# Which pairs of products run in turns, when the token operands are made, and a fifth weight buffer for part of the run

## The chip, the core and the metric

The kernel runs on one core of a Trainium2 chip. The metric is the time of one execution on the device in microseconds (us), the median of several runs. Five engines take part, each with its own queue of instructions that it works off in order: PE (TensorE, matrix products), DVE (VectorE) and ACT (ScalarE) for elementwise work, POOL (GpSimd) and SP (SyncE), which here only issue DMA transfers.

## What is computed

One block of a hybrid encoder, 2048 tokens of 1024 features, all in float32:

```python
h    = rmsnorm(x, norm_g)
proj = h @ W_in            # 1024 -> 6144 columns, 48 column tiles of 128
q, k, v, z_att, gb, gc, u, z_conv, g_att, g_conv = split(proj)
att    = chunked_rel_attention(q, k, v, rel_bias)        # 8 heads, own chunk + 8 before
y_att  = (att * silu(z_att)) @ w_att_out
vconv  = causal_depthwise_conv(gc * u, conv_w, conv_b)   # width 3
y_conv = (gb * vconv * silu(z_conv)) @ w_conv_out
m      = sigmoid(g_att) * y_att + sigmoid(g_conv) * y_conv
out    = rmsnorm(x + m @ w_out, final_norm_g)
```

## The kernel before

**Products.** The tokens are taken in two halves of 1024. The 48 column tiles of `W_in` are taken in 24 *pairs*: 8 gate pairs (numbers 0 to 7), 8 conv pairs (8 to 15), 4 pairs of q and k (16 to 19), 2 of v and 2 of z. A pair on a half is a 2 by 2 block product (two column tiles, two chunks of 512 tokens, and the 1024 features in two blocks of 512), done with seven block products in the place of eight. They are called by the numbers 1, 2, 6, 5, 7, 4, 3, which is the order in `ORDER` (L36). Each needs a *token operand* (a sum or difference of blocks of tokens, made once for a half by `operand_steps`, L348, one of its seven steps for each product number) and a *weight operand* (the same of weight blocks, made for every pair by `operand`, L375). Every operand is split into a high and a low part, ACT making the high one by a cast and DVE the low one by a subtraction (L122 and L123 for weights, L128 and L129 for tokens). `passes` (L132) runs a product as 12 matmuls: for each of four row blocks high by high, high by low, low by high, so that the third matmul is the first that needs the low part of the weights.

**The stages.** The first three pairs of half 0 (`PLAIN`) are computed from tokens that are not normalized yet, as twelve plain groups of 24 matmuls (in the text q0 to q11; L655 on), each scaled afterwards (`scaled`, L605: DVE reads the PSUM tile `ps_p` and frees its bank). Beside them `between` (L630) normalizes the tokens and makes the first five steps of the token operands. Then `seq` (L561 to L564) gives the order of all other products: half 0 pair by pair but for its last two pairs, which run in turns (`ending`), then the first two pairs of half 1 in turns (`beginning`), then the rest. `names` is the order of the pairs, n the place of a pair in it (0 to 23 in half 0, 24 to 47 in half 1). Half 0 splits the weights and stores them (`wc_d`); in half 1 they are loaded from there, but for the three plain pairs, which are split again. The token operands of half 1 are made by the same `operand_steps`, one step two products after the last product that reads the same operand of half 0 (`due`, L776): both halves share 56 slots (`tt`). After pair n = 28 the attention starts (L777): 131 units of it are spread evenly over the products that are left. Then come the two output products.

**What sets the order.** A scheduler lays down each engine's queue when the kernel is built; in the plain stage the order on PE, DVE and ACT is as written (`manual_schedule`, L646). Four buffers hold weight operands (`wr`, L94); one comes free when its product has run and its store to `wc_d` has landed. PSUM has three banks for products (`ps_d`), so a product waits until the product three places ahead has been read out (*evicted*), by ACT for number 1 (L745) and by DVE otherwise (L749 to L769). For v pairs a turn through PE (`vt`, L433) and a split into `vst` (L440 on ACT, L441 on DVE) follow, for q and k a split (L410, L411), for z a SiLU (L453, L454).

## Time and profile before

| What | Value |
|---|---|
| Median of 3 runs | 1554.11 us (1553.26 to 1556.15) |
| The profiled execution, on the device | 1557.6 us |
| Its span, first to last instruction | 1555.8 us |
| PE busy, share of the span | 1516.6 us, 97% |
| DVE busy | 1039.7 us, 67% |
| ACT busy | 680.1 us, 44% |
| Mean granted PE clock | 0.992 of full speed |

PE is busy nearly all the time, so what can be won lies in its waits and in the stretches at a lower clock. In the timeline a row gives start and length; what stands in square brackets is how long the engine had been idle and what ended that.

### The profile page before, as it was taken

Reading aid. Unit: us, or ns where it says so; the run is one execution under the profiler, and the core shown is the slowest. Engines: PE = TensorE matmul, PEld = TensorE weight load, DVE = VectorE, ACT = ScalarE, POOL = GpSimd, SP = SyncE. Lnnn points to the kernel's source line nnn. Section 1 sums busy time; section 2 is a strip of 40 time slices with the busy share of each in tenths; the row PEclk is TensorE's granted clock in tenths of the full one; section 3 lists DMA queues with packets and bytes.
Section 4 is the critical chain, followed back from the end, with each engine's and each line's share of the span. In section 5 each row is a group of like instructions: output and inputs, shape, how many; then the busy total and the mean of one; then the engine's idle time right before and its main releaser. Section 6 shows DMA issues by size and latency. Waiting matters only on the chain.

```text
span 1555.8 us, 21590 instructions
## 1 busy us (share of the span) xinstructions
PE 1516.6 (97%) x7396; PEld 1267.9 (81%) x7396; DVE 1039.7 (67%) x2078; ACT 680.1 (44%) x1250; POOL 155.0 (10%) x294
## 2 busy tenths in 40 slices
PE   9899999999998999999999999999999999999997
PEld 6678888888776788888888888888888888888886
DVE  7977789796668654666666767677755574445544
ACT  6353353443325343555666556666665231112111
POOL 0000000000000001223222222322220000000000
PEclk9999999999999999999999999999999999999999
DMA  5288999988987835999898776888889945365131
GB/s 209 77 285 307 339 353 327 364 310 305 319 301 262 279 122 177 329 339 341 294 290 272 228 265 228 262 261 272 263 278 322 304 162 200 102 233 193 62 109 68
DMA packets 159406, 389.45 MB, mean 250 GB/s; under 512 B 19904, under 2 KB 40384, under 8 KB 159296
## 3 DMA queue, kind: packets, MB, share of 16 engines
q1 hardware_dynamic: 129088, 302.06, 56.2%
q0 software_dynamic: 20992, 69.22, 13.6%
q10 hardware_dynamic: 9216, 16.78, 2.9%
q8 instruction: 59, 0.97, 0.3%
q14 instruction: 51, 0.42, 0.1%
HBM read 236.99 MB, written 150.99 MB: 249 GB/s over the span
## 4 chain that ended last, share of the span: by engine, by line
PE 83%; DVE 9%; ACT 2%; DMA 2%; issue 2%; POOL 0%; SPq 0%; ACTq 0%; DVEq 0%; POOLq 0%
PE ps_d L137 20%; PE ps_d L135 20%; PE ps_d L136 20%; PE ps_d L876 4%; PE ps_d L874 4%; PE ps_d L875 4%; PE ps_s L190 4%; PE po L228 4%; PE ps_t L210 3%; DVE ptl L216 1%; DVE ps_s L196 1%; DMA wc<-wc 1%; DVE xs L304 1%; ACT pr L200 1%; DMA vv<-v 0%
## 5 line engine op out<-in xcount | busy, mean ns | idle before, releaser
L200 ACT ACTIVATE pr<-ps_s,nmax 128x640 f32<-128x640 f32 (+4 forms) x128 | 93.4, 730 | 96.7 <-DVE nmax L196 96.1
L158 POOL DMA_DIRECT2D q<-q x128 | 66.7, 526 | 681.3 <-DVE wc L123 602.5
L196 DVE CUSTOM_DVE_ANT_0 ps_s<-ps_s,bs 128x640 f32<-128x640 f32 (+4 forms) x128 | 95.4, 745 | 53.8 <-PE ps_s L190 53.2
L122 ACT CAST wc<-wraw 128x512 fp32r<-128x512 f32 x120 | 73.6, 621 | 114.2 <-PE ps_d L137 94.2
L202 ACT ACTIVATE pr<-pr,rs 128x640 f32<-128x640 f32 (+4 forms) x128 | 97.8, 764 | 27.3 <-DVE rs L201 27.2
L190 PE MATMUL ps_s<-kk,q 128*128 128x320 f32 (+1 forms) x448 | 97.4, 333 | 2.9 <-ACT pr L200 2.8
L135 PE MATMUL ps_d<-mid,wy 128*128 128x512 f32 x256 | 99.6, 389 | 0.0
L136 PE MATMUL ps_d<-mid,wy 128*128 128x512 f32 x256 | 99.6, 389 | 0.0
L137 PE MATMUL ps_d<-mid,wy 128*128 128x512 f32 x256 | 99.6, 389 | 0.0
L216 DVE TENSOR_TENSOR ptl<-ps_t,pth 128x640 fp32r<-128x640 f32 (+4 forms) x128 | 94.3, 736 | 6.6 <-ACT pth L215 6.0
L215 ACT CAST pth<-ps_t 128x640 fp32r<-128x640 f32 (+4 forms) x128 | 80.0, 625 | 41.0 <-PE ps_t L210 40.0
L123 DVE TENSOR_TENSOR wc<-wraw,wc 128x512 fp32r<-128x512 f32 x120 | 82.2, 689 | 13.7 <-ACT wc L122 13.5
L210 PE MATMUL ps_t<-ident,pr 128*128 128x128 f32 x560 | 83.9, 276 | 1.1 <-DVE ptl L216 0.6
L883 ACT ACTIVATE sq<-y 128x512 f32<-128x512 f32 x32 | 20.2, 632 | 146.0 <-DVE y L878 141.3
L228 PE MATMUL po<-pth,vv 128*128 128x256 f32 x336 | 79.1, 271 | 1.8 <-DMA vv<-v 1.6
L228 PE MATMUL po<-ptl,vv 128*128 128x256 f32 x336 | 78.3, 281 | 0.2 <-DVE ptl L216 0.2
L874 PE MATMUL ps_d<-wo,mh 128*128 128x512 f32 x192 | 74.7, 389 | 0.0
L875 PE MATMUL ps_d<-wo,mh 128*128 128x512 f32 x192 | 74.7, 389 | 0.0
L876 PE MATMUL ps_d<-wo,ml 128*128 128x512 f32 x192 | 74.7, 389 | 0.0
L190 PEld LDWEIGHTS ps_s<-kk,q 128*128 128x128 f32 x448 | 67.0, 190 | 7.8 <-ACT pr L200 7.4
L878 DVE SCALAR_TENSOR_TENSOR y<-ps_d,y 128x512 f32<-128x512 f32 x32 | 22.1, 692 | 76.0 <-PE ps_d L876 75.9
L210 PEld LDWEIGHTS ps_t<-ident,pr 128*128 128x128 f32 x560 | 63.2, 140 | 11.4 <-DVE ptl L216 2.1
(370 smaller groups left out, 4183.8 us busy)
## 6 DMA issues: line engine op xcount, KB each, us to landing
wc<-wc SPq DMA_DIRECT2D x294, 512.0 KB, 4.8
wraw<-wp_in SPq DMA_DIRECT2D x54, 512.0 KB, 5.9
q<-q POOLq DMA_DIRECT2D x128, 128.0 KB, 4.9
gl<-gate SPq DMA_DIRECT2D x64, 256.0 KB, 3.2
mid<-mid SPq DMA_DIRECT2D x64, 256.0 KB, 5.2
bs<-bias POOLq DMA_DIRECT2D x32, 320.0 KB, 7.2
gate<-c ACTq DMA_DIRECT2D x34, 256.0 KB, 4.7
v<-vst SPq DMA_DIRECT2D x64, 128.0 KB, 4.7
```

Of the source, the lines that this page charges most:

```text
L135: nc.tensor.matmul(ps, lhsT=w[:, 0, k, :], rhs=rh[:, cs], start=(first and k == 0), stop=False)
L136: nc.tensor.matmul(ps, lhsT=w[:, 0, k, :], rhs=rl[:, cs], start=False, stop=False)
L137: nc.tensor.matmul(ps, lhsT=w[:, 1, k, :], rhs=rh[:, cs], start=False, stop=(last and k == len(rhs) - 1))
L190: nc.tensor.matmul(ps[:, i, :m], lhsT=q[s][:, g * P:(g + 1) * P], rhs=kk[:, k1 - n + i * m:k1 - n + (i + 1) * m], start=(s == 0), stop=(s ...
L196: nc.vector.tensor_tensor_reduce(out=view, in0=view, in1=bv, scale=-0.125, scalar=3.0e38, op0=ALU.add, op1=ALU.min, accum_out=nmax)
L200: nc.scalar.activation(out, view, AF.Exp, bias=nmax, scale=-1.0, accum_out=rs)
L210: nc.tensor.transpose(out=ps[:, j * P:(j + 1) * P], in_=pr[:, j * P:(j + 1) * P], identity=ident)
L216: nc.vector.tensor_sub(lo[:, js, qs], src, hi[:, js, qs].bitcast(F32))
L228: nc.tensor.matmul(ps[:, (g0 + a) * P:(g0 + b) * P], lhsT=vv[:, g0 + j, :], rhs=s[:, j, a * P:b * P], start=(i == 0 and s is pt[0]), stop= ...
L874: nc.tensor.matmul(ps, lhsT=mh[:, gs], rhs=wh, start=(k == 0), stop=False)
L875: nc.tensor.matmul(ps, lhsT=mh[:, gs], rhs=wl, start=False, stop=False)
L876: nc.tensor.matmul(ps, lhsT=ml[:, gs], rhs=wh, start=False, stop=(k == KT - 1))
```

## The change

Six things change.

First, the order of half 0: gate pairs 4 and 5 move ahead of the conv pairs, and the last two gate pairs stand behind the first two couples of conv pairs, so that four conv pairs now follow each other at the end. In half 1 gate pair 5 comes at the start, with 3 and 4.

Second, the pairs that run in turns: in half 0 no longer the last two but the first two behind the plain products (n = 3 and 4), and at the start of half 1 three in the place of two (`BEGIN`).

Third, the token operands of half 0: two steps stay in the plain stage (at q6 and q7), and the other five are made beside the pairs in turns, one before every second product.

Fourth, those of half 1: `due` is now a list of places counted from the change of halves (product -5, -4, -1, 2, 5, 7 and 11), and their temporary `t1` comes from the pool of weight sums.

Fifth, a fifth weight buffer: from n = 16 to n = 38 every fifth weight operand is put in an extra pool (`more`), and operands are made or loaded three products ahead there, also in half 0. The memory is that of the convolution's tiles (`cva`), which are opened only while conv pairs run. Ahead of that the same memory holds one raw weight tile (`extra`), since two pairs in turns need more raw tiles at a time; raw tiles of pair 4 are requested at the start.

Sixth, the attention starts one pair later (n = 29), and the pool for gates opens one pair later.

```diff
+BEGIN = 3
-    wtile = lambda name: wr.tile([P, 2, 4, P], F32R, tag="w", name=name)
+    ring = [0, wr]
+
+    def wtile(name):
+
+        ring[0] += 1
+        w = ring[1] if ring[0] % 5 == 0 else wr
+        return w.tile([P, 2, 4, P], F32R, tag="w", name=name)
...
-    conv_stack = ExitStack()
-    cva = conv_stack.enter_context(tc.tile_pool(name="cva", bufs=2))
+    spare = ExitStack()
+    extra = spare.enter_context(tc.tile_pool(name="extra", bufs=1))
+    pools = []
...
-                    t1 = e("t1")
+                    t1 = s_pool.tile([P, 4, P], F32, tag="s1", name="t1").rearrange("p k c -> p (k c)") if half else e("t1")
...
-        r = ww.tile([P, 2, 4, P], F32, tag="w", name="wraw")
+        r = (extra if (p, n) == (names[PLAIN + 2], 0) else ww).tile([P, 2, 4, P], F32, tag="w", name="wraw")
...
-    order = [[*range(G, G + 4), *conv_gate(G + 4, G + 5, G + 6, G + 7), *range(Q, Q + 8)]]
-    order.append([G + 3, G + 4, *range(G, G + PLAIN), *range(Q, Q + 8), *conv_gate(), G + 5, G + 6, G + 7])
+    order = [[*range(G, G + 6), *conv_gate(G + 6, G + 7), *range(Q, Q + 8)]]
+    order.append([G + 3, G + 4, G + 5, *range(G, G + PLAIN), *range(Q, Q + 8), *conv_gate(), G + 6, G + 7])
...
-    both = [(i, k) for i in (6, 5, 7, 4, 3) for k in range(2)]
-    ending = [(1, 0), (2, 0), (6, 0), (1, 1), (2, 1), (6, 1), *both[2:]]
-    beginning = [(1, 0), (2, 0), (1, 1), (2, 1), *both]
-    mid0, mid1 = names[PLAIN:NPAIR - 2], names[NPAIR + 2:]
-    seq = [(p, i) for p in mid0 for i in ORDER]
-    seq += together(*names[NPAIR - 2:NPAIR], ending)
-    seq += together(*names[NPAIR:NPAIR + 2], beginning)
-    seq += [(p, i) for p in mid1 for i in ORDER]
+    beginning = [(i, k) for k in range(BEGIN) for i in (1, 2)]
+    beginning += [(i, k) for i in (6, 5) for k in range(BEGIN)]
+    beginning += [(i, k) for k in range(BEGIN) for i in (7, 4)]
+    beginning += [(3, k) for k in range(BEGIN)]
+    seq = together(names[PLAIN:PLAIN + 2], [*((i, k) for k in range(2) for i in (1, 2)), *((i, k) for i in ORDER[2:] for k in range(2))])
+    seq += [(p, i) for p in names[PLAIN + 2:NPAIR] for i in ORDER]
+    change = len(seq)
+    seq += together(names[NPAIR:NPAIR + BEGIN], beginning)
+    seq += [(p, i) for p in names[NPAIR + BEGIN:] for i in ORDER]
+    due = [change + d for d in (-5, -4, -1, 2, 5, 7, 11)]
...
+    for k in range(2):
+        load_raw(4, k)
...
-        if q > 5 and len(built) < 5:
+        if q in (6, 7):
             built.append(next(steps))
...
+        if n == PLAIN + 3 and i == 1:
+            spare.close()
+            pools[:] = [spare.enter_context(tc.tile_pool(name="cva", bufs=2))]
+        if n == 16 and i == 1:
+            spare.close()
+            ring[1] = spare.enter_context(tc.tile_pool(name="more", bufs=1))
+        elif n == NPAIR + BEGIN + PLAIN + 8 and i == 1:
+            ring[1] = wr
+            spare.close()
+            pools[:] = [spare.enter_context(tc.tile_pool(name="cva", bufs=2))]
...
-        ahead = 3 if half else 2
+        ahead = 3 if half or ring[1] is not wr else 2
...
-        if half == 0 and len(built) < 7 and s:
+        if half == 0 and len(built) < 7 and s % 2:
             built.append(next(steps))
```

How the queues read at the three places that the prediction speaks of. A row is the line, the operation, and the tile written and the tiles read; the numbers in the names tell tiles of one name apart.

**DVE in the plain stage.** Before, from the read-out of q5 (`c_980`) to the first low part of the weights of q9 (`w0_1041`):

```order
L607 TENSOR_TENSOR c_980<-ps_p_891,rb_836 128x512
L123 TENSOR_TENSOR w0_984<-wraw_538,w0_984 128x512
L123 TENSOR_TENSOR w0_987<-wraw_538,w0_987 128x512
L607 TENSOR_TENSOR plain_763<-plain_763,rb_909 128x512
L607 TENSOR_TENSOR plain_823<-plain_823,rb_909 128x512
L129 TENSOR_TENSOR t20l_1018<-xs_523,t20h_1017 128x512
L129 TENSOR_TENSOR t21l_1022<-xs_523,t21h_1021 128x512
L129 TENSOR_TENSOR t22l_1026<-xs_523,t22h_1025 128x512
L129 TENSOR_TENSOR t23l_1030<-xs_523,t23h_1029 128x512
L607 TENSOR_TENSOR c_1033<-ps_p_933,rb_909 128x512
L123 TENSOR_TENSOR w0_1041<-wraw_540,w0_1041 128x512
```

In the changed kernel the same read-out (`c_984`) is followed by one more sum of tokens, then by the same rows down to `t20l`; from there to the first low part of the weights of q9 (`w0_1045`):

```order
L364 TENSOR_TENSOR xs_517<-xs_517,xs_528 128x512
L137 TENSOR_TENSOR t21l_1026<-xs_523,t21h_1025 128x512
L401 TENSOR_TENSOR s2_1251<-s1_1250,wraw_542 128x512
L137 TENSOR_TENSOR t22l_1030<-xs_523,t22h_1029 128x512
L406 TENSOR_TENSOR wraw_544<-wraw_542,wraw_544 128x512
L137 TENSOR_TENSOR t23l_1034<-xs_523,t23h_1033 128x512
L622 TENSOR_TENSOR c_1037<-ps_p_937,rb_913 128x512
L366 TENSOR_TENSOR xs_523<-xs_523,xs_517 128x512 x2
L137 TENSOR_TENSOR t60l_1207<-xs_517,t60h_1206 128x512
L366 TENSOR_TENSOR xs_523<-xs_523,xs_517 128x512 x2
L137 TENSOR_TENSOR t61l_1212<-xs_517,t61h_1211 128x512
L131 TENSOR_TENSOR w0_1045<-wraw_540,w0_1045 128x512
```

The read-out of q6 (`c_1033`, now `c_1037`) stands thirteenth behind that of q5 where it was ninth, and the low part of q9's weights twentieth where it was tenth; the steps for `t5` and `t7`, which stood between the read-outs of q7, q8 and q9, have moved behind the plain stage.

**ACT at the end of the q and k pairs.** Before, in the last of these pairs (n = 19): `hi` is the split of a result, `wc_4043`, `wc_4062` and `wc_4083` are the weights of its products 7, 4 and 3, `wc_4106` those of the next pair's product 1:

```order
L122 CAST wc_4043<-wraw_3820 128x512
L410 CAST hi_4103<-c22_4100 128x512
L122 CAST wc_4062<-wraw_3820 128x512
L122 CAST wc_4083<-wraw_3818 128x512
L122 CAST wc_4106<-wraw_3986 128x512
L410 CAST hi_4124<-u_4016 128x512
```

In the changed kernel (`wc_4030`, `wc_4056`, `wc_4074` are the weights of 7, 4 and 3, `wc_4095` those of the next pair's product 1; `v_4093` is the result of product 3):

```order
L130 CAST wc_4030<-wraw_3837 128x512
L130 CAST wc_4056<-wraw_3837 128x512
L130 CAST wc_4074<-wraw_3835 128x512
L420 CAST hi_4115<-c22_4112 128x512
L420 CAST hi_4136<-u_4028 128x512
L420 CAST hi_4166<-v_4093 128x512
L130 CAST wc_4095<-wraw_4003 128x512
L130 CAST wc_4118<-wraw_4003 128x512
```

The weights of product 4 no longer stand behind the split of product 7's result; the weights of the next pair's product 1 now stand behind the split of product 3's.

**DVE at the change of halves.** Before, in the two z pairs at the end of half 0 (`wc_4766`, `wc_4786` and `wc_4833` are weights of their products 7 and 4):

```order
L129 TENSOR_TENSOR t63l_4763<-xs_1594,t63h_4762 128x512
L123 TENSOR_TENSOR wc_4766<-wraw_4522,wc_4766 128x512
L123 TENSOR_TENSOR wc_4786<-wraw_4321,wc_4786 128x512
L760 TENSOR_TENSOR c22_4803<-v_4744,ps_d_4789 128x512
L761 TENSOR_TENSOR u_4557<-u_4557,ps_d_4789 128x512
L360 TENSOR_TENSOR t1_4809<-xs_1603,xs_1594 128x512
L454 SCALAR_TENSOR_TENSOR sz_4806<-sz_4806,c22_4803 128x512
L360 TENSOR_TENSOR t1_4815<-xs_1603,xs_1594 128x512
L129 TENSOR_TENSOR t50l_4812<-t1_4809,t50h_4811 128x512
L360 TENSOR_TENSOR t1_4821<-xs_1603,xs_1594 128x512
L129 TENSOR_TENSOR t51l_4818<-t1_4815,t51h_4817 128x512
```

In the changed kernel the steps for `t5` and `t7` stand in half 1, ahead of the read-out of the second of its products (`c11_4965`, from bank `ps_d_4951`):

```order
L366 TENSOR_TENSOR xs_1590<-xs_1590,xs_1587 128x512
L137 TENSOR_TENSOR t52l_4984<-t1_4981,t52h_4983 128x512
L370 TENSOR_TENSOR t1_4987<-xs_1596,xs_1587 128x512
L366 TENSOR_TENSOR xs_1590<-xs_1590,xs_1587 128x512 x2
L137 TENSOR_TENSOR t53l_4990<-t1_4987,t53h_4989 128x512
L137 TENSOR_TENSOR t70l_5047<-xs_1593,t70h_5046 128x512
L137 TENSOR_TENSOR t71l_5051<-xs_1593,t71h_5050 128x512
L137 TENSOR_TENSOR t72l_5055<-xs_1593,t72h_5054 128x512
L777 TENSOR_TENSOR c11_4965<-u_4947,ps_d_4951 128x512
L137 TENSOR_TENSOR t73l_5059<-xs_1593,t73h_5058 128x512
```

Between the read-out of the last pair's product 7 (`c22_4862`) and `c11_4965` stand 27 other instructions of this size on DVE. No split of weights is among those behind the last three products of half 0.

## Rows read from the trace of the kernel before

**Rows 1.** Waits of PE: line, waited for, us in total, times, longest.

```profile
PE ps_p L135 <- DVE c L607: 9.1, 3, 3.6
PE ps_d L137 <- DVE wc L123: 6.0, 4, 3.6
PE ps_s L190 <- ACT pr L200: 2.8, 8, 0.6
```

**Rows 2.** Timeline of PE, plain stage: the three waits, two neighbouring matmuls.

```profile
60.09 0.47 PE L135 MATMUL ps_p<-rawh,w 128*128 128x512 f32 x1 [2.46 <-DVE c L607]
...
61.07 0.63 PE L135 MATMUL ps_p<-rawh,w 128*128 128x512 f32 x1
61.50 0.63 PE L136 MATMUL ps_p<-rawl,w 128*128 128x512 f32 x1
...
76.00 0.50 PE L135 MATMUL ps_p<-rawh,w 128*128 128x512 f32 x1 [3.07 <-DVE c L607]
...
85.34 0.79 PE L135 MATMUL ps_p<-rawh,w 128*128 128x512 f32 x1 [3.61 <-DVE c L607]
```

**Rows 3.** Windows: length, busy us of PE, PEld, DVE, ACT, POOL; PEclk, DMA share, GB/s.

```profile
60.00:65.00 5.00, 4.91 (x14) 3.81 (x15) 5.00 (x9) 1.75 (x3) 0.00 (x0) 0.66 0.50 159
...
75.00:80.00 5.00, 4.00 (x18) 3.32 (x19) 2.91 (x6) 2.50 (x4) 0.00 (x0) 1.00 0.42 157
...
85.00:90.00 5.00, 4.66 (x11) 3.69 (x12) 4.75 (x9) 4.68 (x9) 0.00 (x0) 0.50 0.91 297
90.00:95.00 5.00, 5.00 (x20) 3.98 (x20) 2.05 (x4) 2.05 (x4) 0.00 (x0) 0.85 0.93 234
...
410.00:420.00 10.00, 7.97 (x27) 5.83 (x27) 5.77 (x9) 2.18 (x4) 0.00 (x0) 0.83 0.91 349
```

**Rows 4.** Timeline of DVE, plain stage: read-outs of q5 and q6.

```profile
59.25 0.69 DVE L607 TENSOR_TENSOR c<-ps_p,rb 128x512 f32<-128x512 f32 x1
...
64.65 0.70 DVE L607 TENSOR_TENSOR c<-ps_p,rb 128x512 f32<-128x512 f32 x1
```

**Rows 5.** Timeline of PE from the q, k pairs to the v pairs.

```profile
415.12 0.50 PE L135 MATMUL ps_d<-t40h,wc 128*128 128x512 f32 x1 [1.95 <-ACT wc L122]
...
438.80 0.50 PE L137 MATMUL ps_d<-t40h,wc 128*128 128x512 f32 x1 [1.53 <-DVE wc L123]
...
442.75 0.50 PE L137 MATMUL ps_d<-t30h,wc 128*128 128x512 f32 x1 [0.49 <-DVE wc L123]
```

**Rows 6.** Timeline of ACT: a weight cast behind a split; the two splits of `vt`.

```profile
413.93 0.62 ACT L410 CAST hi<-c 128x512 fp32r<-128x512 f32 x1 [7.01 <-DVE c L760]
414.45 1.66 ACT L122 CAST wc<-wraw 128x512 fp32r<-128x512 f32 x3
...
470.43 0.37 ACT L440 CAST vst<-vt 128x256 fp32r<-128x256 f32 x1 [0.49 <-DVE vst L441]
```

**Rows 7.** Timeline of PE at the change of halves.

```profile
493.85 0.50 PE L135 MATMUL ps_d<-t70h,wc 128*128 128x512 f32 x1 [1.31 <-ACT wc L122]
...
504.37 0.73 PE L137 MATMUL ps_d<-t40h,wc 128*128 128x512 f32 x1 [3.60 <-DVE wc L123]
...
521.34 0.59 PE L135 MATMUL ps_d<-t10h,wc 128*128 128x512 f32 x1 [1.95 <-DMA wc<-wc]
```

**Rows 8.** Windows at the change of halves, columns as in rows 3.

```profile
490.00:500.00 10.00, 8.32 (x36) 6.11 (x35) 10.00 (x18) 4.67 (x8) 0.00 (x0) 1.00 0.46 179
500.00:510.00 10.00, 6.40 (x22) 4.82 (x21) 8.42 (x15) 5.60 (x10) 0.00 (x0) 0.83 0.83 286
...
520.00:530.00 10.00, 8.66 (x31) 7.04 (x32) 5.54 (x9) 3.21 (x6) 0.00 (x0) 0.83 0.58 193
```

**Rows 9.** Windows of two conv pairs of half 0, n = 13 and 14, columns as in rows 3.

```profile
284.35:303.40 19.05, 19.05 (x86) 15.78 (x85) 12.90 (x21) 9.29 (x22) 0.00 (x0) 1.00 1.01 380
303.40:322.45 19.05, 19.05 (x86) 15.78 (x85) 18.04 (x45) 7.41 (x13) 0.00 (x0) 1.00 0.90 334
```

**Rows 10.** Groups of DVE, 322.45 to 341.50 (n = 15): busy us, mean ns, idle us.

```profile
L304 DVE SCALAR_TENSOR_TENSOR xs<-xs,ng_sb,rb 128x512 f32<-128x512 f32 x8 | 5.7, 750 | 0.0
```

More of the change, by code (lines that the diff above doesn't have):

```diff
@@ L469, in conv @@
         def conv(c, x, y):
-            a = cva.tile([P, 2 + CH], F32, tag="a", name="cva")
+            a = pools[0].tile([P, 2 + CH], F32, tag="a", name="cva")
             av[c] = a
@@ L551, in make_c, with together @@
         return raw_w(wy[i, d]), [gate(i, d, c) for c in (2 * hf, 2 * hf + 1)]
-    def together(p, q, order):
-        return [((p, q)[k], i) for i, k in order]
-    both = [(i, k) for i in (6, 5, 7, 4, 3) for k in range(2)]
-    ending = [(1, 0), (2, 0), (6, 0), (1, 1), (2, 1), (6, 1), *both[2:]]
-    beginning = [(1, 0), (2, 0), (1, 1), (2, 1), *both]
-    mid0, mid1 = names[PLAIN:NPAIR - 2], names[NPAIR + 2:]
-    seq = [(p, i) for p in mid0 for i in ORDER]
-    seq += together(*names[NPAIR - 2:NPAIR], ending)
-    seq += together(*names[NPAIR:NPAIR + 2], beginning)
-    seq += [(p, i) for p in mid1 for i in ORDER]
+    def together(pairs, order):
+        return [(pairs[k], i) for i, k in order]
+    beginning = [(i, k) for k in range(BEGIN) for i in (1, 2)]
[8 more added lines that the diff above has]
+    due = [change + d for d in (-5, -4, -1, 2, 5, 7, 11)]
     fslot = lambda name: slot(name, F32)
@@ L706, in block_kernel @@
     turned = None
-    due = []
     uv = {}
@@ L714, in block_kernel @@
             due.pop(0)
+            if turned is None:
+                for _ in x1:
+                    pass
+                turned = operand_steps(1)
             next(turned)
-        if half == 0 and i == 1 and n + 1 < NPAIR:
+        if n == PLAIN + 3 and i == 1:
[8 more added lines that the diff above has]
+            pools[:] = [spare.enter_context(tc.tile_pool(name="cva", bufs=2))]
+        if half == 0 and i == 1 and PLAIN < n < NPAIR - 1:
             for k in range(2):
                 load_raw(names[n + 1], k)
-        elif i == 1 and n in (NPAIR, *range(NPAIR + 2, NPAIR + 1 + PLAIN)):
+        elif i == 1 and n in (NPAIR, *range(NPAIR + BEGIN, NPAIR + BEGIN - 1 + PLAIN)):
             for k in range(2):
-                load_raw(names[max(n, NPAIR + 1) + 1], k)
-        ahead = 3 if half else 2
+                load_raw(names[max(n, NPAIR + BEGIN - 1) + 1], k)
+        ahead = 3 if half or ring[1] is not wr else 2
         while nw < min(len(seq), s + ahead + 1):
@@ L770, in block_kernel @@
             ev[0](g1, 1, v)
-        if n == NPAIR - 1:
-            if turned is None:
-                for _ in x1:
-                    pass
-                turned = operand_steps(1)
-            due.append(s + 2)
-        elif n == NPAIR + 1 + PLAIN and i == 3:
+        if n == NPAIR + BEGIN - 1 + PLAIN and i == 3:
             first.close()
@@ L785, in block_kernel @@
                 at_stages += 1
-        if n == NPAIR + 2 + PLAIN + 16 and i == 1:
-            conv_stack.close()
+        if n == NPAIR + BEGIN + PLAIN + 16 and i == 1:
+            spare.close()
             gp = pool("gp", 5)
```

## The prediction

> **What bounds the kernel now.** I read the table of waits of PE first, since PE is busy for 97% of the span: what can be won is its waits and what the clock loses behind them. The waits gather in few groups [rows 1]. The largest, 9.1 us in three waits, is the plain stage: a group of matmuls waits until DVE has read out the group three places ahead. The 6.0 us on low weight parts lie, by the timeline, where the q and k pairs end and where the halves change. The attention's waits for `pr` are 2.8 us in eight short pieces.
>
> Then the timeline of PE at each place, with the windows around it for the clock. A matmul takes 19.05 / 84 = 0.227 us at full clock (a pair is 7 products of 12 matmuls and fills a window of 19.05 us exactly, [rows 9]), so a product takes 2.72 us, a plain group of 24 takes 5.44 us. [...] By a window's granted clock g, (1 - g) of its length is lost: 1.7 us in 60 to 65, 2.5 in 85 to 90, 0.75 in 90 to 95, 1.7 in 410 to 420, nothing in 75 to 80 [rows 3].
>
> So the kernel loses, by place: **plain stage** 2.46 + 3.07 + 3.61 = 9.1 us of waits [rows 2] and 1.7 + 2.5 + 0.75 = 4.95 of clock, 14.1 together; **end of q and k** 1.95 + 1.53 + 0.49 = 4.0 [rows 5] and 1.7 of clock, 5.7; **change of halves** 1.31 + 3.60 + 1.95 = 6.9 [rows 7] and 1.7 + 1.7 of clock [rows 8], 10.3. The change touches all three, and nothing else in it can win much: between them PE runs without a gap.
>
> **Plain stage.** DVE's operations follow each other every 0.60 us there: the read-out of q5 starts at 59.25, that of q6, nine places on, at 64.65 [rows 4]. Up to the read-out of q5 the queue of DVE does not change in length, so q8's wait of 2.46 us and its 1.7 of clock stay; one added sum of tokens delays q8's low weights by one place, 0.3 us taken (between 0 and 0.6). Two steps of token operands and their sums have left the stretch behind; those that stay now stand ahead of q9's weights. By the queue shown with the change, the read-out of q6 starts at 59.25 + 13 x 0.60 = 67.05, the first low part of q9's weights at 59.25 + 20 x 0.60 = 71.25 instead of 65.25. q8 runs from 60.09, 5.44 + 1.7 + 0.3 us, so q9 starts at 67.5 and wants the low part with its third matmul at about 68.1 to 68.4; it gets it near 72.0. That is a new wait of 3.6 us, and I take 1.7 of clock behind it, as after the first one. The read-outs of q7 and q8 follow at once (two and three places on, 72.45 and 73.05 ready within 1 us), long before q10 and q11 want their banks, so the waits of 3.07 and 3.61 go. Left: 2.46 + 1.7 + 0.3 + 3.6 + 1.7 = 9.8 against 14.1, a gain of 4.3. Ends: 9.6, if q9 waits for nothing because DVE runs these rows faster; 2.8, if the clock behind q9's wait costs 3.25 as at 85.34.
>
> **The first pairs in turns.** Five operand steps (four casts on ACT and four subtractions on DVE each, and sums) now lie beside n = 3 and 4, 38.1 us of PE. DVE is busy for only 2.05 of 5 us in 90 to 95 [rows 3], and each operand serves two products in a row, so a step has 5.4 us where its four subtractions and up to four sums of 0.60 take 2.4 to 4.8; the extra raw tile lets the second pair's weights come in time. Taken: 0. Bound: two pairs in turns with token steps between them exist before, at the end of half 0, and lost 3.60 + 1.7 there [rows 7, 8], so 0 to 5.3 us lost; no gain, since PE has no wait to give back there. I take 0 since in that stretch DVE was full (10.00 of 10, [rows 8]), and here it is not.
>
> **The order of the conv pairs.** Gate pairs leave the places between the conv pairs, so the last four conv pairs follow each other. In the couple n = 13 and 14 DVE was busy for 12.90 + 18.04 = 30.9 us of 38.1, and PE never waited [rows 9]. By the order of the changed kernel, eight normalizations of half 1's tokens lie beside the last couple, where they lay beside a gate pair; with their 5.7 us [rows 10] DVE has 36.6 of 38.1. It just fits: 0, with an end of 4 us lost, no gain where PE had no gap.
>
> **The fifth buffer and the end of q and k.** Three products ahead, the weights of product 4 no longer stand behind the split of product 7's result, and the waits of 1.95, 1.53 and 0.49 go. But ACT works in order, and its queue shows the same fault one place on: the weights of the next pair's product 1 stand behind the split of `v_4093`, the result of product 3, which runs immediately ahead of it. Before, a split and the casts behind it, at 413.93 and 414.45 [rows 6], made PE wait 1.95 us; I take the same 1.95 and 1.7 of clock. At the change from the first v pair to the second the weights of product 1 stand behind both `vst` splits of a tile that was turned just ahead: cast 0.37, DVE's part 0.49, cast 0.37 [rows 6], and then the weights' own cast 1.66 / 3 = 0.55, together 1.8 us that PE waits. Left: 1.95 + 1.7 + 1.8 = 5.5 against 5.7, a gain of 0.2. Ends: a gain of 5.7 if DVE hands over early enough; a loss of 3, if the second wait is as long as 3.1 and followed by half clock too.
>
> **The change of halves.** The token steps that stood between the weights of the z pairs are gone from there, and the weights no longer wait for stores of the ring at that place: the 1.31, the 3.60 and the 1.95 go, with 3.4 of clock. What is late next is the read-outs. The result of the last pair's product 7 (`c22_4862`) comes 5 x 2.72 = 13.6 us after that pair's start, and is read from 14.3 on; `c11_4965`, 28 places behind at 0.60, starts at 31.1 and ends at 31.8. Its bank is wanted three products after the second of half 1, at 11 x 2.72 = 29.9: a wait of 1.9 us, and one of 0.55 for the next read-out two products on. With 1.7 of clock for the first, 4.2 are left of 10.3, a gain of 6.1. Ends: 10.3, nothing left; 2.7, if the wait is 3.60 as at 504.37 and both are followed by half clock (10.3 - 3.6 - 0.55 - 3.4).
>
> **Attention.** Its 131 units lie over 126 products in place of 133, 5% denser, so its waits of 2.8 us [rows 1] grow by 0.2; the end is 2.8 lost, if they double.
>
> **Clock.** Of the waits of 1.9 us and over, those of 2.46, 3.61, 1.95, 3.60 and 1.95 were followed by a window below full clock, the one of 3.07 was not, nor was that of 1.31 [rows 2, 3, 5, 7, 8]. So I charge 1.7 for each wait from 1.9 on, none for that of 1.8. [...]
>
> **Sum.** 4.3 + 0 + 0 + 0.2 + 6.1 - 0.2 = 10.4 us. The profiled execution took 1557.6 us on the device (span 1555.8), 3.5 above the median of the runs; 1557.6 - 10.4 = 1547.2, less 3.5 gives **1543.7**.
>
> **The rivals.** *The new waits don't come.* DVE overtakes: q9's weights and the read-outs at the start of half 1 are in time. For it: the 0.60 us spacing is a count of a queue that never waits for its inputs, and both waits are small beside the 12 and 16.8 us of queue that they rest on. Against: those queues have grown, not shrunk, and a wait for inputs only makes them later. Gains 9.6 + 0.2 + 10.3 - 0.2 = 19.9: 1534.2.
>
> *The plain stage gives nothing back.* q9's wait is as long as the two removed, with their clock: DVE's sums wait for ACT's casts `t21h` to `t60h` that stand between them, 4.3 us longer. For it: five casts stand in the stretch. Against: ACT was busy for only 1.75 of 5 us in 60 to 65 [rows 3]. Time: 1548.0.
>
> *Every wait pays the clock.* The 1.8 us at the v pairs is followed by half clock like the 1.95: 1.7 more, 1545.4. For it: 1.95 paid twice; against: 3.07 paid nothing.
>
> *The change doesn't do what it says.* The waits at both ends of the weights' queue only move: the change of halves keeps its 10.3 us, that is 6.1 lost, and the plain stage gives nothing, 4.3 lost: 1554.1, no change.
>
> *Slower: four conv pairs in a row.* The second conv pair of a couple has DVE busy for 18.04 of 19.05 us [rows 9], and a gate pair behind it used to take up what was left over. If DVE needs 3.6 us more than PE in each of the four, because read-outs queue behind the convolution's sums, 14.4 us are lost: 1558.1. It decides from (10.4 + 3.1) / 4 = 3.4 us a pair on. Against: the two couples together have 30.9 + 36.6 = 67.5 us of DVE work in 76.2, and this would need 90.6.
>
> **How the numbers follow.** This kernel's measurement can tell about 0.2%, 3.1 us, from no change: faster is below 1551.0, slower above 1557.2. The forecast, 1538 to 1547.5, has 0.42; every wait pays 0.15; the new waits don't come 0.20 (1531 to 1538); the plain stage gives nothing 0.13 (1547 to 1551); no change 0.06; slower 0.04. Faster is 0.42 + 0.15 + 0.20 + 0.13 = 0.90. The range from 1534 to 1550 leaves out half of the second case (0.10), no change and slower, 0.20 in all.
>
> **What would show it.** In the profile after: the group waits for DVE's read-outs fall from 9.1 us to near 2.5, and a wait for DVE's `w` of about 3.6 appears in the plain stage near 72; the first product in turns starts 4.3 us earlier; one wait of about 1.9 for ACT's `wc` at the first v pair, and one of 1.8 at the second; at the start of half 1 a wait of 1.9 for a `c` of DVE, and no wait for stored weights. I am wrong if the low weights of q9 come before 69, if PE waits in n = 3 and 4 or n = 12 to 15, or if the attention's waits for `pr` exceed 5.6.

## The result and the profile after

The changed kernel takes 1559.91 us (median of 7 runs, 1553.99 to 1563.89), the kernel before 1554.11 us in the same comparison; the ratio is 1.0040 (95% interval 1.0023 to 1.0057). It is slower by 0.4%, where 1543.7 was forecast and 1534 to 1550 given as the range. The profiled execution took 1559.99 us on the device, its span is 1558.2 us, 2.4 above that of before. In experiments 1 and 5 one of the ten executions each ran at a granted clock of 0.59 and 0.56 and took 2390 and 2532 us; the medians there include it, the ratios do not.

The gain that was forecast is there, and it was lost again in places that the sum had at nothing. A table by stage shows it. Each entry is the start of the first matmul of that place in PE's timeline, as the difference from the kernel before (its own times are in the first row), so a negative number is a lead in us. At n = 29 no unit of the attention has run in any of the kernels.

| | n = 3 | n = 8 | n = 10 | n = 19 | n = 23 | n = 29 | first output product | span |
|---|---|---|---|---|---|---|---|---|
| before | 93.8 | 189.0 | 227.1 | 399.4 | 486.9 | 612.8 | 1198.7 | 1555.8 |
| after | -3.6 | -3.6 | +5.3 | +5.3 | +5.0 | -3.9 | -0.5 | +2.4 |

So the plain stage gives 3.6 us and the change of halves 8.8; n = 8 and 9 lose 8.9, the attention 3.4 and the output products 2.8.

The table of waits of PE after (line, waited for, us in total, times, longest), to be read against [rows 1]:

```profile
PE ps_d L143 <- DVE c L777: 4.7, 2, 4.1
PE ps_d L143 <- ACT wc L130: 4.2, 2, 2.4
PE ps_p L145 <- DVE w L131: 4.1, 3, 3.4
PE ps_p L143 <- DVE c L622: 3.9, 2, 2.5
PE po L236 <- DMA vv<-v: 3.2, 2, 2.2
PE ps_t L218 <- DVE ptl L224: 3.1, 3, 2.7
...
PE ps_d L143 <- DVE part L842: 1.8, 3, 0.9
...
PE ps_s L198 <- ACT pr L208: 1.1, 3, 0.5
```

The first row, the sixth and the one for `part` had no counterpart of that size before. The low weight parts of `ps_d`, 6.0 us before, are gone.

**Plain stage.** PE's timeline (start, length, idle time ahead of it and what ended that), where [rows 2] showed three waits:

```profile
60.25 0.47 PE L143 MATMUL ps_p<-rawh,w 128*128 128x512 f32 x1 [2.46 <-DVE c L622]
61.36 0.50 PE L145 MATMUL ps_p<-rawh,w 128*128 128x512 f32 x1 [0.41 <-DVE w L131]
68.07 0.47 PE L143 MATMUL ps_p<-rawh,w 128*128 128x512 f32 x1 [1.42 <-DVE c L622]
72.19 0.80 PE L145 MATMUL ps_p<-rawh,w 128*128 128x512 f32 x1 [3.42 <-DVE w L131]
```

The waits of q10 and q11 are gone, and q9 waits for its weights until 72.2. The windows (length, busy us of PE, PEld, DVE, ACT and POOL, granted clock, DMA share, GB/s) show the clock:

```profile
60.00:65.00 5.00, 4.34 (x18) 3.31 (x19) 5.00 (x10) 4.48 (x8) 0.00 (x0) 1.00 0.56 174
...
70.00:75.00 5.00, 2.81 (x7) 2.23 (x8) 5.00 (x9) 1.22 (x2) 0.00 (x0) 0.50 0.28 64
75.00:80.00 5.00, 5.00 (x20) 4.06 (x19) 1.96 (x4) 0.04 (x1) 0.00 (x0) 0.85 0.40 157
```

**n = 8 and 9** (a gate pair and the first pair of the second couple of conv pairs). PE's timeline:

```profile
203.98 0.47 PE L143 MATMUL ps_d<-t30h,wc 128*128 128x512 f32 x1 [1.07 <-DVE v L784]
...
221.92 0.76 PE L143 MATMUL ps_d<-t70h,wc 128*128 128x512 f32 x1 [4.10 <-DVE c L777]
```

Both times, and in a third wait of 0.59 us, a read-out by DVE ends it, and behind the longest PE goes on at the lower clock, as this window shows (columns as above):

```profile
220.00:225.00 5.00, 3.08 (x7) 2.48 (x8) 4.72 (x9) 2.60 (x6) 0.00 (x0) 0.50 1.04 413
```

Why DVE is late is seen by following the longest wait back: DVE's timeline, SP's, ACT's, and SP's table of waits in that stretch.

```profile
219.76 0.69 DVE L400 TENSOR_TENSOR s<-wraw 128x512 f32<-128x512 f32 x1 [3.23 <-DMA wraw<-wp_in]
220.49 0.69 DVE L401 TENSOR_TENSOR s<-s,wraw 128x512 f32<-128x512 f32 x1
221.10 0.68 DVE L777 TENSOR_TENSOR c<-u,ps_d 128x512 f32<-128x512 f32 x1
```

```profile
207.25 0.93 SPq L409 DMA_DIRECT2D wc<-wc  x1
213.71 0.84 SPq L383 DMA_DIRECT2D wraw<-wp_in  x2
```

```profile
206.78 0.33 ACTq L415 DMA_DIRECT2D gate<-c  x1
```

```profile
SPq L383 <- DMA gate<-c: 5.5, 1, 5.5
```

DVE is idle for 3.23 us ahead of a sum of raw weights of n = 10, since these have not landed; the read-out that PE needs stands two places behind that sum, at 221.10, and the last matmul of its product started at 212.00. SP issued the load of these weights at 213.71, after 5.5 us in which it waited for a store of gates to land; ACT had issued that store at 206.78, between the squares of half 1's tokens. That this landing is what held SP is inferred by the profile from the order of events. The wait of 1.07 us is of the same kind: DVE stands idle for 4.45 us ahead of a tile of `bias` that has not landed, with the read-out behind it.

**q, k and v, change of halves.** PE's timeline:

```profile
426.32 0.50 PE L143 MATMUL ps_d<-t10h,wc 128*128 128x512 f32 x1 [2.37 <-ACT wc L130]
...
450.39 0.50 PE L143 MATMUL ps_d<-t10h,wc 128*128 128x512 f32 x1 [1.84 <-ACT wc L130]
...
521.43 0.50 PE L143 MATMUL ps_d<-t20h,wc 128*128 128x512 f32 x1 [1.85 <-ACT u L773]
```

The waits of [rows 5] have moved to the first product of the v pairs, and at the change of halves 1.85 us are left of those in [rows 7].

**Half 1.** PE in the attention and at its end, and DVE at that end:

```profile
729.15 0.36 PE L236 MATMUL po<-pth,vv 128*128 128x256 f32 x1 [2.22 <-DMA vv<-v]
...
1192.01 0.77 PE L218 MATMUL ps_t<-ident,pr 128*128 128x128 f32 x5 [2.71 <-DVE ptl L224]
```

```profile
1188.05 0.69 DVE L131 TENSOR_TENSOR wy<-wraw,wy 128x512 fp32r<-128x512 f32 x1 [4.33 <-DMA wraw<-wy]
```

The pattern is that of n = 9: the first weights of the output products have not landed, ACT stands for 3.87 us and DVE for 4.33 us at them, and the attention's `pth` on ACT and `ptl` on DVE, which PE wants, stand behind.

### The profile page after: what moved, and what is told of

Same layout as the page of the kernel before. It is cut to its first block, busy times and chain, and to the rows that moved or that the text cites. A ratio compares the mean times of both kernels' runs of the same rounds, so it can differ in the third digit from the quotient of the medians.

```text
span 1558.2 us, 21575 instructions
## 1 busy us (share of the span) xinstructions
PE 1515.1 (97%) x7396; PEld 1265.2 (81%) x7396; DVE 1037.8 (67%) x2078; ACT 678.1 (44%) x1250; POOL 155.1 (10%) x294
## 4 chain that ended last, share of the span: by engine, by line
PE 81%; DVE 7%; DMA 5%; issue 4%; ACT 2%; SPq 1%; POOL 0%; DVEq 0%; ACTq 0%; POOLq 0%
PE ps_d L145 19%; PE ps_d L143 19%; PE ps_d L144 19%; PE po L236 4%; PE ps_d L897 4%; PE ps_d L898 4%; PE ps_d L896 4%; PE ps_s L198 3%; PE ps_t L218 3%; DMA wraw<-wy 1%; PE ps_p L145 1%; DVE xs L314 1%; PE ps_p L143 1%; PE ps_p L144 1%; DVE ps_s L204 1%
```

## The experiments

Stages and rows are those of one profiled execution of each kernel; the times are medians, and a ratio is to the kernel before, timed beside it, with its 95% interval. The leads of all kernels, measured as above:

| | n = 3 | n = 8 | n = 10 | n = 19 | n = 23 | n = 29 | first output product | span |
|---|---|---|---|---|---|---|---|---|
| after | -3.6 | -3.6 | +5.3 | +5.3 | +5.0 | -3.9 | -0.5 | +2.4 |
| gate stores by POOL | -9.3 | -9.3 | -8.1 | -8.1 | -8.6 | -17.4 | -8.6 | -5.6 |
| half 1's tokens from n = 9 | -4.3 | -4.2 | -4.2 | -4.0 | -6.1 | -15.0 | -13.6 | -10.7 |
| gate pairs later | -3.1 | -3.1 | -1.5 | -1.5 | -2.5 | -10.0 | -8.9 | -6.3 |
| q9's weights first | -4.4 | -4.4 | +0.8 | +0.8 | +0.4 | -8.5 | -4.6 | -0.7 |
| half 1 as before | -3.5 | -3.5 | +5.3 | +5.3 | +4.9 | -3.9 | -5.0 | -5.0 |
| four buffers | -3.4 | -3.4 | 0.0 | +3.9 | +1.6 | -7.1 | +0.2 | +4.1 |
| steps in the plain stage | -1.4 | -1.4 | +3.6 | +3.6 | +3.2 | -5.5 | -4.7 | -2.8 |
| POOL and n = 9 | -9.5 | -9.5 | -9.5 | -9.5 | -13.3 | -20.8 | -14.2 | -11.2 |
| these and half 1 as before | -9.3 | -9.3 | -9.3 | -9.3 | -11.5 | -20.3 | -18.7 | -18.4 |
| n = 9 and half 1 as before | -3.9 | -3.9 | -3.9 | -3.6 | -7.4 | -15.0 | -11.3 | -11.3 |

The theory at this point: DVE, SP and ACT work in order (in the rows above DVE's read-out starts at 221.10, behind the sum that had to wait until 219.76), and in n = 8 the gate pair's stores, the first loads of half 1's tokens and the loads of raw weights hold each other up. The rival was that of the prediction: conv pairs too dense for DVE.

**1. Gate stores of half 0 by POOL.**

```diff
-            nc.scalar.dma_start(gate_d[i][d][g], t)
+            (nc.gpsimd if g < 2 else nc.scalar).dma_start(gate_d[i][d][g], t)
```

> Only the queue that issues the stores of gates in half 0 is changed: POOL in the place of ACT. In the changed kernel PE loses 8.9 us in n = 8 and 9 against before: the raw weights for n = 10 are issued 5.5 us late (213.71), because SP waits for a gate store to land, DVE then waits 3.2 us for these weights, and the read-out that PE wants stands behind. Theory (a queue blocked by gate stores): the 4.1 us wait in n = 9 and its 2.5 us of clock go, the loss in n = 8 and 9 falls from 8.9 to 2 to 3.5 us, the time by 5 to 6.5 us. Rival (DVE has too much to do beside two conv pairs, 18.94 of 19.04 us in n = 7): the loss stays within 1 us of 8.9. Second rival (the transfers are at their limit, 0.95 of the DMA engines in n = 9): the raw weights are as late as before, the loss stays near 8.9.

1549.99 us, ratio 0.9967 (0.9948 to 0.9987). The loss from n = 8 to 10 falls from 8.9 to 1.1 us, where 2 to 3.5 was expected, SP no longer waits ahead of the raw weights, and this is what is left in PE's timeline there:

```profile
210.68 0.47 PE L143 MATMUL ps_d<-t70h,wc 128*128 128x512 f32 x1 [0.85 <-DVE c L777]
```

Both rivals expected no change. What was not expected: the plain stage gives 9.3 us in the place of 3.6. The stores of the twelve plain groups are gone from ACT's queue there, and the queues come out in another order, in which q9's weights stand ahead of the third operand step. In PE's timeline q9's only wait is

```profile
68.56 0.50 PE L145 MATMUL ps_p<-rawh,w 128*128 128x512 f32 x1 [0.41 <-DVE w L131]
```

In the second half 8.8 of the 17.4 us are lost again, most of them in one place, where values of the attention land late:

```profile
736.15 0.55 PE L236 MATMUL po<-pth,vv 128*128 128x256 f32 x1 [6.35 <-DMA vv<-v]
```

**2. The normalization of half 1's tokens one pair later.**

```diff
-        if half == 0 and 8 <= n < 22 and i in (2, 5, 4):
+        if half == 0 and 9 <= n < 22 and i in (2, 5, 4):
```

> Only the start of the normalization of half 1's tokens is changed, from n = 8 to n = 9; its loads of tokens (256 KB each) and the squares on ACT then don't lie beside the gate pair n = 8. Theory (a queue blocked by gate stores that ACT issues late between squares): gates are stored earlier, SP isn't held, the loss in n = 8 and 9 falls from 8.9 us to under 3, and no equal loss comes in n = 9 to 11. Rival (DVE has too much to do beside two conv pairs): squares are on ACT, so the loss stays within 1 us of 8.9. Second rival (transfers at their limit): 2.5 MB less in n = 8 and 9, some 7 us of transfer at 350 GB/s, the loss falls too, but comes back one pair later.

1549.72 us, ratio 0.9973 (0.9958 to 0.9989). From n = 8 to 10 nothing is lost, and 0.3 us from n = 10 to 19, which speaks against the limit of the transfers as well as against DVE's load. DVE still waits for the raw weights of n = 10, and longer than in the changed kernel, and the same read-out stands behind, now four places. DVE's timeline, then PE's:

```profile
210.42 0.69 DVE L400 TENSOR_TENSOR s<-wraw 128x512 f32<-128x512 f32 x1 [4.91 <-DMA wraw<-wp_in]
...
212.96 0.68 DVE L777 TENSOR_TENSOR c<-u,ps_d 128x512 f32<-128x512 f32 x1
```

```profile
214.68 0.39 PE L143 MATMUL ps_d<-t70h,wc 128*128 128x512 f32 x1
```

But the wait ends 6.6 us after the start of n = 9, where it ended 13.0 us after it in the changed kernel, and so the read-out is through before PE wants its bank. So the late transfer, for which DVE waited 4.91 us, cost PE nothing here. At the start of the v pairs the wait of 2.37 us and its clock became one of 0.93.

**3. The last two gate pairs later**, at n = 10 and 13, four conv pairs in a row at n = 6 to 9.

```diff
-    order = [[*range(G, G + 6), *conv_gate(G + 6, G + 7), *range(Q, Q + 8)]]
+    order = [[*range(G, G + 6), *range(C, C + 4), G + 6, C + 4, C + 5, G + 7, C + 6, C + 7, *range(Q, Q + 8)]]
```

> Only the order of pairs in half 0 is changed: the last two gate pairs stand at n = 10 and 13 in the place of n = 8 and 11, so that four conv pairs stand at the start and two at the end. Theory (gate stores and the start of the token loads meet at n = 8): the loss in n = 8 and 9 falls from 8.9 us to under 3. Rival (conv pairs are too dense for DVE): four in a row from n = 6 make DVE late earlier, the loss in n = 8 to 10 is 8.9 us or more.

1554.83 us, ratio 1.0001 (0.9978 to 1.0024). Four conv pairs in a row cost nothing up to n = 9, and what is lost up to n = 10, 1.6 us, is mostly one wait in n = 9, with no gate pair yet, ended by a square of half 1's tokens on ACT:

```profile
217.32 0.47 PE L143 MATMUL ps_d<-t70h,wc 128*128 128x512 f32 x1 [1.35 <-ACT xt L303]
```

The density of conv pairs is out: DVE was busy for 18.90 of 19.04 us in the second of these pairs, as this window of the same kernel shows, and PE did not wait.

```profile
166.84:185.88 19.04, 19.04 (x85) 15.77 (x84) 18.90 (x37) 6.89 (x12) 0.00 (x0) 1.00 0.75 265
```

All kernels together show the same link. With none of the edits of 1 to 3 (the changed kernel and experiments 4 to 7) SP issues the raw weights of n = 10 from 3.4 to 6.9 us after the start of n = 9, and the loss from n = 8 to 10 is 3.4 to 8.9 us. With one or two of them it issues them between 4.6 us ahead of that start and the start itself, and the loss is 0 to 1.6. Before, it was 5.8 us ahead, and nothing was lost.

**4. q9's weights first.** In the plain stage they are split ahead of the second operand step.

```diff
                 now, late = late, []
+                if q == 7:
+                    for k in range(2):
+                        weights0(p + 1, n, k)
                 between(q)
...
-            if c and p + 1 < PLAIN:
+            if c and p + 1 < PLAIN and q != 7:
...
-            elif c and n == 0:
+            elif c and n == 0 and p + 1 == PLAIN:
```

> Only the place of the weights of the last plain pair's second column tile is changed: they are split ahead of the second operand step, not behind it. In the changed kernel q9 waits 3.4 us for them and runs 2.0 us longer at half clock, behind a wait of 1.4 for the read-out of q6. Theory (the order of DVE alone makes q9 late): the first product in turns starts at 84.5 to 86.5 in the place of 90.25, and the time falls by 4 to 5.5 us. Rival (DVE's work in the stretch is the bound, and the wait goes to the read-outs or to the weights of the first product in turns): it starts after 88.5, the time falls by under 2 us.

1557.83 us, ratio 1.0026 (1.0002 to 1.0051); the first product in turns starts at 89.37, 0.9 earlier. As the rival has it, the wait goes to the read-out. PE, then DVE:

```profile
70.36 0.76 PE L143 MATMUL ps_p<-rawh,w 128*128 128x512 f32 x1 [3.93 <-DVE c L622]
```

```profile
68.32 0.69 DVE L400 TENSOR_TENSOR s<-wraw 128x512 f32<-128x512 f32 x1 [1.21 <-DMA wraw<-wp_in]
...
69.53 1.88 DVE L622 TENSOR_TENSOR c<-ps_p,rb 128x512 f32<-128x512 f32 x3
```

Four rows of weights now stand ahead of q6's read-out, and a sum of raw weights of a later pair, which the scheduler had put into the gap, waited 1.21 us for its transfer there. That DVE's work is the bound, the rival's reason, does not follow: in experiment 1 the weights of q9 stand behind that read-out and ahead of the third operand step, and the first product in turns starts at 84.55.

**5. Half 1 as before**: two pairs in turns at its start, the attention from n = 28.

```diff
-BEGIN = 3
+BEGIN = 2
...
-    order.append([G + 3, G + 4, G + 5, *range(G, G + PLAIN), *range(Q, Q + 8), *conv_gate(), G + 6, G + 7])
+    order.append([G + 3, G + 4, *range(G, G + PLAIN), *range(Q, Q + 8), *conv_gate(), G + 5, G + 6, G + 7])
```

> Half 1 alone goes back to the order of before: two pairs in turns at its start, three gate pairs at its end, the attention from n = 28. Theory (what half 1 loses comes from the attention and the conv pairs lying closer to the end): from n = 25 to the first output product before gains nothing and the changed kernel lost 3.4 us, by a wait of 2.7 us and 2.4 of clock at 1188.9 behind the weights of the output products and by 3.2 us of waits for values; the output products lost 2.9 more. With the old order both are back near before: 1 us or less from n = 25 to the first output product, under 1 us behind it, the time 3.5 to 6 us lower. Rival (these are waits for transfers that differ from execution to execution): the waits stay, the time falls by under 2 us. At the change of halves the first theory says nothing.

1551.63 us, ratio 0.9983 (0.9970 to 0.9997). Up to n = 29 it goes as the changed kernel does, to 0.2 us; from there to the first output product it gains 1.1 us where the changed kernel lost 3.4, and behind that nothing is lost (0.0 against 2.8). The wait of 2.71 us at the end of the attention is one of

```profile
1189.62 0.39 PE L236 MATMUL po<-ptl,vv 128*128 128x256 f32 x1 [0.48 <-DVE ptl L224]
```

and PE's table has no wait for `part` any more. The third pair in turns gives nothing at the change of halves (8.8 us with it and without). The edit undoes three things at once, the third pair in turns, the place of its gate pair and the later start of the attention; their shares are not parted.

**6. Four weight buffers throughout.**

```diff
-            ring[1] = spare.enter_context(tc.tile_pool(name="more", bufs=1))
...
-        ahead = 3 if half or ring[1] is not wr else 2
+        ahead = 3 if half else 2
```

> The fifth weight buffer is left out, and operands in half 0 are made two products ahead throughout. In the changed kernel n = 19 to 25 gained 9.2 us against before (from 5.34 behind to 3.85 ahead). Theory (the gain comes from the moved token steps, since the waits there were for weights behind these steps): the gain of n = 23 to 25 (9.5 us) stays to within 2 us, and the waits at n = 19 to 21 change by under 2. Rival (the fifth buffer makes it): the gain falls under 4 us, with waits for stores or loads of weights at the change of halves.

1563.63 us, ratio 1.0083 (1.0051 to 1.0115). The gain from n = 23 to 29 stays, 8.7 us, so it does not come from the fifth buffer, nor, by experiment 5, from the third pair in turns. What is left is the moved token steps, as the theory has it, and the last two pairs of half 0, which no longer run in turns; no run parts these two. The waits of the q and k pairs are those of before, and two of 1.95 us in the place of one; at the change of halves the wait for a stored weight is there again, shorter:

```profile
396.10 0.50 PE L143 MATMUL ps_d<-t40h,wc 128*128 128x512 f32 x1 [1.95 <-ACT wc L130]
...
419.02 0.50 PE L143 MATMUL ps_d<-t40h,wc 128*128 128x512 f32 x1 [1.95 <-ACT wc L130]
...
515.87 0.47 PE L143 MATMUL ps_d<-t10h,wc 128*128 128x512 f32 x1 [1.51 <-DMA wc<-wc]
```

From n = 10 to 23 it loses 1.6 us where the changed kernel gains 0.4, so in these two profiles the fifth buffer is worth 2.0 us, little more than the lower clock behind a single wait cost (1.6 to 1.8, see the end). The rest of its time was lost in the attention, 7.2 us.

**7. Five steps in the plain stage**, as before; the pairs in turns stay.

```diff
-        if q in (6, 7):
+        if q > 5 and len(built) < 5:
             built.append(next(steps))
```

> All of the first five operand steps stand in the plain stage again, as before; the pairs in turns stay. Theory (the steps in the plain stage make the read-outs of q7 and q8 late): the first product in turns starts at 93 to 95 in the place of 90.25, the waits of some 3 us for q10 and q11 are back, the time is 2.5 to 4.5 us higher where nothing else changes. Rival (moving steps gained nothing, since q9's wait took its place): it starts at 90 to 91.

1557.61 us, ratio 1.0029 (1.0010 to 1.0049). The first product in turns starts at 92.38, 2.1 us later than in the changed kernel, less than expected; two waits for read-outs are back:

```profile
75.88 0.80 PE L143 MATMUL ps_p<-rawh,w 128*128 128x512 f32 x1 [4.68 <-DVE c L622]
...
85.22 0.56 PE L143 MATMUL ps_p<-rawh,w 128*128 128x512 f32 x1 [2.28 <-DVE c L622]
```

So the move alone gives 2.1 us, since q9's new wait takes the rest. The median is no higher than that of the changed kernel: this profile lost 5.0 us in n = 8 and 9 and 0.8 in the attention, where the other lost 8.9 and 3.4, and the timed runs scatter by as much.

**8. The edits of 1 and 2 together.**

> Both edits that took the loss at n = 8 and 9 away, together: gate stores of half 0 by POOL, the normalization of half 1's tokens from n = 9. In the run with POOL the first product in turns started at 84.55, since ACT no longer issues eight stores there and DVE's queue has the weights of q9 behind the read-out of q6, not behind the third operand step. Theory: the two add up: 9 us ahead of before at the first product in turns, nothing lost in n = 8 and 9, 13 to 18 us ahead at n = 25, and 1544 to 1549 as a median. Rival (the second half gives it back, as the waits for values of 6.4 us did in the run with POOL): ahead by as much at n = 25, but 1549 or more.

1546.47 us, ratio 0.9943 (0.9919 to 0.9968). Nothing is lost from n = 3 to 19, the lead at n = 29 is 20.8 us (as at n = 25, for which 13 to 18 was expected), since the waits at the start of the v pairs are shorter too (13.3 us ahead at n = 23); 6.6 are lost in the attention and 3.0 behind it. That is the theory for half 0 and the rival for half 1, with the median in the theory's range.

**9. These and half 1 as before**, and **10. the edit of 2 and half 1 as before**, gate stores on ACT.

> The two edits of the combined run and the old order of half 1 (two pairs in turns at its start, the attention from n = 28). Theory (the losses of the changed kernel are three, and each has its own cause): 20 us ahead of before at n = 25 as in the combined run, no loss from there to the end, where the combined run lost 6.6 us in the attention and 3.0 in the output products: a span of 1534 to 1538 and a median of 1537 to 1541. Rival (what is won in half 0 is lost in the waits for values of the attention whatever its start): some 6 us are lost there again, a median of 1544 or more.

> As the run before it, but the stores of gates stay on ACT: the normalization of half 1's tokens from n = 9 and the old order of half 1. Theory: no loss in n = 8 and 9, q9's wait and its clock stay (4 to 6 us), so the span is 4 to 6 us above that of the run with POOL as well, and the median 1541 to 1546. Rival (POOL's stores cost as much later as they give in the plain stage): within 2 us of it.

The ninth takes 1539.0 us, ratio 0.9908 (0.9883 to 0.9933), faster than the kernel before and, by its median, than the changed one. The theory holds, with a span of 1537.4; from n = 29 to the end it loses 1.9 us where it expected nothing. PE's table of waits shows what is left:

```profile
PE po L236 <- DMA vv<-v: 3.6, 3, 1.6
PE ps_s L198 <- ACT pr L208: 2.8, 8, 0.6
PE ps_p L143 <- DVE c L622: 2.5, 1, 2.5
PE ps_d L143 <- ACT wc L130: 1.8, 1, 1.8
PE ps_d L143 <- ACT u L773: 1.7, 1, 1.7
```

The tenth takes 1545.31 us, ratio 0.9949 (0.9931 to 0.9966). Its span is 7.1 above the ninth's, a little over the 4 to 6 expected: 5.4 in the plain stage, where q9's waits are back, and 2.0 in the attention by a wait for values of 2.8 us. The rival, by which POOL's stores cost as much later as they give, is out.

## Why the prediction was wrong

By its own steps, against the profiled execution (a gain is positive):

| Step | forecast | measured |
|---|---|---|
| plain stage | 4.3 | 3.6 |
| first pairs in turns | 0 | 0.0 |
| order of the conv pairs | 0 (to -4) | -8.9 |
| end of q and k | 0.2 | 0.4 |
| change of halves | 6.1 | 8.8 |
| attention | -0.2 (to -2.8) | -3.4 |
| behind it | not in the sum | -2.8 |
| sum | 10.4 | -2.4 |

**What held.** The plain stage lost 2.46 + 0.41 + 1.42 + 3.42 = 7.7 us of waits and 2 us of clock, near the 9.8 of the sum, with q9's weights where they were expected (72.2, forecast 72.0). Two of the items differ and make up for each other: q8 did not lose its 1.7 us of clock, was through earlier, and PE then waited 1.42 us for q6's read-out, which DVE started at 67.25 (forecast 67.05). DVE's queue set the time, as the prediction had it. At the v pairs the two waits were 2.37 and 1.84, forecast 1.95 and 1.8, at the places that were read from ACT's queue. Half clock came behind the first (matmuls 0.43 us apart from 428.23 to 430.79, a granted clock of 0.81 in 425 to 430) and not behind the second (1.00 in 450 to 455). That is as charged, but luck: the last section shows the second wait with the lower clock.

At the change of halves one wait of 1.85 came where 1.9 was forecast, and its size is luck too, for it is another wait. It lies one product earlier and ends with ACT's read-out of a product 1, which stands behind casts of token operands; these wait for sums that DVE makes:

```profile
519.75 0.62 ACT L136 CAST t53h<-t 128x512 fp32r<-128x512 f32 x1 [2.39 <-DVE t L370]
...
520.80 0.58 ACT L773 COPY u<-ps_d 128x512 f32<-128x512 f32 x1
```

DVE's read-out, on which the forecast rests, started where it was expected, 31.3 us after the start of the last pair (forecast 31.1):

```profile
523.19 0.68 DVE L777 TENSOR_TENSOR c<-u,ps_d 128x512 f32<-128x512 f32 x1
```

PE, held by the wait before, came to its bank only at 524.28. So operand steps ahead of a read-out were the right cause, in the wrong queue. No second wait and no loss of clock came; that is most of the 2.7 us by which this step was too small.

**What failed** is the step on the order of the conv pairs, which stands in the sum with 0 and cost 8.9 us. It asked only whether DVE's work fits beside the products, 36.6 of 38.1 us, and it looked at n = 12 to 15, where indeed nothing was lost. The change also moved a gate pair to n = 8, where the loads of half 1's tokens begin: in the changed kernel eight such loads, the stores of gates and the raw weights of the next pairs pass through the queues of SP and ACT there, and before, the same eight loads lay beside a conv pair. The prediction read the queues of PE, DVE and ACT at the places that it named, and SP's nowhere. Experiments 1 and 2 each take one of the parties away, and the loss goes from 8.9 to 1.1 and to 0; experiment 3 moves the gate pair away and leaves 1.6, with four conv pairs in a row. None of the signs that the prediction named for being wrong came (q9's weights at 72.2, no wait in n = 3 and 4 nor in n = 12 to 15, 1.1 us for `pr`): they watched the places that the sum already had. The rival that was to end slower had the right sign and the wrong mechanism: DVE at 18.90 of 19.04 us cost PE nothing in experiment 3.

**Attention and what is behind it.** The sum let the waits for `pr` grow by 5%, with 2.8 us as the bound. They fell from 2.8 to 1.1 us; what was lost instead are the waits for values (3.2 us) and the one of 2.71 us for `ptl`. That 3.4 us lies near the bound is luck. The 2.8 us behind the attention were not in the sum. Both losses go with the changes to half 1, which experiment 5 undoes together and has both back. For the output products this is clear: eight kernels with three pairs in turns lose 1.9 to 3.9 us there, three with two pairs 0.0 to 0.3. For the attention it is likely but not shown: eight with three lose 0.8 to 8.8, 4.2 in the mean, three with two gain 1.1 or lose up to 3.6, 1.4 in the mean, and the two ranges overlap.

**What stays open.** Why SP's load of raw weights waits for the landing of a gate store, 5.5 us in the changed kernel, is not shown by any run; that it does so rests on the profile's inference and on experiments 1 and 2, in which the wait is gone from this stretch. Nor is it shown why values of the attention land late by 0.4 us in one execution and 6.4 in another, or by which of its parts the change to half 1 costs the output products 2.8 us. As single waits differ so much, kernels that differ by 2 us in a stage can't be ranked by their medians alone.

## What to carry to other kernels

When pairs or tiles change places, list for each new neighbour what it issues on every queue, the DMA queues of SP and ACT too, and look for the first place where two streams of transfers begin together. In n = 9 DVE had time to spare (busy for 16.36 of 25.63 us) and still made PE wait 4.10 us, since an instruction in its queue waited 3.23 us for a transfer and the read-out behind it came too late; ask when the transfer lands and when PE wants the bank, not only how busy the engine is. Signs of being wrong should also watch the steps that the sum has at nothing. Undo each part of a change by itself: here the token steps that left the plain stage were worth keeping (2.1 us, experiment 7), the third pair in turns was not, and the best kernel also has two small edits that belong to no part of the change.

## What was not expected of the hardware

The same wait at the same place did not always cost clock. q8 waited 2.46 us in the changed kernel and 2.47 in the ninth experiment's; the window 60 to 65 had a granted clock of 1.00 in the first, as shown above, and 0.66 in the second:

```profile
60.00:65.00 5.00, 4.85 (x14) 3.79 (x15) 5.00 (x9) 2.90 (x5) 1.63 (x3) 0.66 0.55 197
```

At the second v pair ten of the eleven new kernels wait 1.84 us. Behind it PE goes on at full clock in four of them, as in the changed kernel (1.00, first row), and at a lower one for a while in six, as in experiment 1 (0.66, second row). There the wider spacing of the matmuls (0.43 us between 439.20 and 439.63 in experiment 2, 0.23 us at full clock) costs 1.6 to 1.8 us:

```profile
450.00:455.00 5.00, 4.51 (x21) 3.41 (x22) 2.57 (x5) 2.05 (x5) 0.00 (x0) 1.00 0.64 202
```

```profile
435.00:440.00 5.00, 4.70 (x15) 3.79 (x16) 2.17 (x4) 0.77 (x2) 0.00 (x0) 0.66 0.67 209
```

In the changed kernel a lower clock stood behind the waits of 3.42 us (0.50 in 70 to 75) and 4.10 us (0.50 in 220 to 225). Behind the 3.07 us of before none did (1.00, [rows 3]), and for 1.84 and 2.46 us it came out both ways. A charge by the length of the wait, as in the sum, was therefore right on some waits by chance.
